# Delta rule: the block transfers begun by GpSimd pair by pair, the merges 19 turns later, more buffers for the inverse and its input

## The chip, the core and the metric

The kernel runs on one core of one Trainium2 chip. TensorE (PE) does the matrix products, VectorE (DVE), ScalarE (ACT) and GpSimd (POOL) work element by element, and SyncE (SP) begins transfers and computes nothing. Every engine executes its own instructions strictly in the order in which the program lists them, and waits where an input is not there or a buffer is not free. A transfer runs by itself once an engine has issued it. The metric is the time of one execution in device microseconds (us).

## The reference, cut to what is concerned

The program is a decoder of four layers followed by a second block of two layers. Layers 0 and 3 mix the tokens with a gated delta rule, the others with differential attention and a gated linear recurrence. The change touches the delta rule alone.

```python
def gated_deltanet(u, valid, w_in, conv_w, a_log, dt_bias, norm_w, w_out):
    proj = u @ w_in                     # [.., 1024] -> q, k, v, z: 4 x 1024, beta and a: 8 each
    qkv = jax.nn.silu(causal_depthwise_conv(proj[..., :DN_CONV_CH], conv_w))
    ...
    o = chunk_gated_delta_rule(q, k, v, beta, g)      # 8 heads of 128
    o = rmsnorm(o, norm_w) * jax.nn.silu(z)
    return o.reshape(b, L, DN_V) @ w_out

def chunk_gated_delta_rule(q, k, v, beta, g):
    ...
    a_strict = jnp.where(strict, jnp.einsum("nbhid,nbhjd->nbhij", kb, kc) * decay, 0.0)
    m = a_strict + jnp.eye(CHUNK, dtype=f32)
    u = lax.linalg.triangular_solve(m, vc * bc[..., None], left_side=True,
                                    lower=True, unit_diagonal=True)
    w = lax.linalg.triangular_solve(m, kb * jnp.exp(gc)[..., None], left_side=True,
                                    lower=True, unit_diagonal=True)
    def step(state, xs):                # along the chunks of the sequence
        v_new = ui - jnp.einsum("bhid,bhde->bhie", wi, state)
        o = (jnp.einsum("bhid,bhde->bhie", qi * jnp.exp(gi)[..., None], state)
             + jnp.einsum("bhij,bhje->bhie", attn, v_new))
        ...
```

For each head and each chunk of the sequence a unit triangular matrix `m` has to be inverted (or solved with), and then a state runs along the chunks.

## The kernel before

**The layout.** The sequence has 272 columns: 16 tokens ahead and two blocks of 128. The kernel works with one triangular matrix of 128 by 128 for each head and block, and one of 16 by 16 for the tokens ahead. The eight heads go in four pairs, p = 0 to 3.

**The big products.** The projections to k, v, q and z come as 16 pieces of weights (`_dn`, `DN_ORDER`: k0 k1 v0 q0 k2 v1 q1 k3 z0 v2 q2 v3 q3 z1 z2 z3, where the digit is the pair). `chunk` (L411) loads a piece: SP issues the transfer `wraw` (L415), ACT casts it to a high part `whi` (L418), and DVE subtracts to get the low part `wlo` (L421). `wraw`, `whi` and `wlo` have three buffers each. `mm3` then multiplies each piece in three passes (high by high, low by high, high by low) with 272 columns: these are the large matmuls `pm`, 48 of a piece.

**The small work** of a pair is a task, a Python generator that emits a few instructions and yields. After every eight large matmuls all tasks are asked once; call this a turn. A task that yields n is left alone for n turns. Where a line says `while ...: yield`, the task waits at build time until another task has come so far. Once all is emitted, a scheduler sets the final order on each engine; each engine executes in that order.

A pair goes through these tasks:

- `dn_keys` begins when k of the pair is projected. It works out the decays (`E`, `Dx`, `Dm`) and norms, has PE multiply k by k (`ga`, `gm`, and `ssq` for the norms), and DVE scales the result into `U`, the five triangular matrices of the pair (four of 128 by 128, and those of the 16 tokens ahead). `U` is held in `fx`, fixed buffers made once per stage in `dn_fixed`, with `At`, `vm`, `km` and the inverse `Y`.
- `dn_blocks` inverts the 40 blocks of 16 by 16 on the diagonals. `U` goes to memory (`ud`, L940), the 40 blocks come back one per partition (`X`, L942), and POOL solves them: 15 steps, each a multiply (L952) and a subtract (L953), and a copy (L954) into `yb`. `yb` goes to memory (`yd`, L957) and comes back spread as `U` is (`yc`, L959). SP issues all four transfers.
- `dn_merge` builds the full inverse from those blocks, by 16 to 32 to 64 to 128. DVE masks `yc` into `Ym` and `yw`; PE multiplies (`gp`, then `pp`, three times); DVE and ACT carry the results between them (`gcm`, `gs`, `yt`) and write them into `Y`. The result is `inv[p]`.
- `dn_chain` begins when q of the pair is projected, and from `inv[p]` on runs the state `St` along the chunks (`ksp`, `pv`, `spn`, `po`). `dn_tail` and `proj_out` then normalise, gate by z and project.

The yields set when the steps are emitted: `ud` and `X`, 6 turns on the solve, 10 turns on `yd` and `yc`, 8 turns on the merge, if the pairs before have come far enough (`solved` counts the pairs whose chain has read its inverse). Pair 2 and 3 further wait with their `U` for the inverse two pairs back, because `U` has two buffers, and the merge of p waits until the chain of p-1 has read `Y`, of which there is one.

The changed functions stand below as they are before.

Of the kernel before, what the change touches and what calls it, by code (L numbers as in the profile page):

```python
# [9 lines left out]
F32 = mybir.dt.float32  # L10
# [7 lines left out]
P = 128  # L18
# [3 lines left out]
T = NM + NX  # L22
# [278 lines left out]
class Prog:  # L301
# [232 lines left out]
    def _dn(self, s, layer, last, e):  # L534
# [14 lines left out]
        self.solved = 0  # L549
# [73 lines left out]
    def dn_fixed(self):  # L623

        d1, V = self.d1, self.V
        self.fx = []
        for i in range(2):
            t = dict(U=d1.tile([P, 5, P], F32, name=f"U{i}"), At=d1.tile([48, 48], F32, name=f"Atm{i}"),
                     vm=d1.tile([48, P], F32, name=f"vm{i}"), km=d1.tile([48, 2, P], F32, name=f"km{i}"),
                     Y=d1.tile([P, 4, P], F32, name="Y") if i == 0 else self.fx[0]["Y"])  # L630
            V.memset(t["U"][:, 4, :], 0.0)
            for n in ("At", "vm", "km"):
                V.memset(t[n], 0.0)
            self.fx.append(t)
# [117 lines left out]
    def dn_ssq(self, x, out):  # L752

        sp = self.pst("ssq2")
        self.V.memset(sp[:, 4:5], 0.0)
        sq = self.d2.tile([P, 2, T], F32, tag="sq2", name="sq2", bufs=1)
        self.act(sq, x, AF.Square)
        for h, c in self.M4:
            i = 2 * h + c
            self.colsum(sp[:, i:i + 1], sq[:, h, self.CK[1 + c]])  # L760
        for h in range(2):
            self.mm(sp[self.RH[h], 4:5], sq[:, h, 0:16], self.ones[:, 0:1])
        self.V.tensor_scalar_add(out=out, in0=sp[:, 0:5], scalar1=EPS)

    def dn_keys(self, p, kT, gates, ready, keys):
# [3 lines left out]
        while not ready.done:  # L769
            yield  # L770
        rows, bet, gc, ng = gates
        fx = self.fx[p % 2]
# [26 lines left out]
        while p > 1 and self.inv[p - 2] is None:  # L799
            yield  # L800
        U = fx["U"]
# [12 lines left out]
        yield from self.dn_blocks(U, box)  # L814
        while p and self.solved < p:
            yield
        self.inv[p] = yield from self.dn_merge(U, box[0], fx["Y"])

    def dn_chain(self, p, kT, vT, qT, gates, keys, outs, last):
# [4 lines left out]
        fx = self.fx[p % 2]  # L824
# [44 lines left out]
        for h in range(2):  # L869
# [3 lines left out]
            act(vm[r], kp[r, 3, :], AF.Copy, scale=sk[r, 4:5])  # L873
        while self.inv[p] is None:
            yield
# [59 lines left out]
    def dn_blocks(self, U, box):  # L935

        d2, dd, V, G = self.d2, self.dd, self.V, self.G
        q = self.nc.sync
        ud = dd.tile([5, 129, P], F32, tag="ud", name="ud")
        q.dma_start(out=ud[:, 0:P, :].rearrange("m p c -> p m c"), in_=U)  # L940
        X = d2.tile([40, 16, 16], F32, tag="X", name="X", bufs=1)
        q.dma_start(out=X, in_=bass.AP(ud.tensor, ud.offset, [[2064, 40], [P, 16], [1, 16]]))  # L942
        yb = d2.tile([40, 16, 2, 16], F32, tag="yb", name="yb", bufs=1)
        yield 6
# [10 lines left out]
        yield 10  # L955
# [4 lines left out]
        box.append(yc)  # L960
        yield 8
# [979 lines left out]
```

## Time and profile before

| | |
|---|---|
| Time, median of 3 runs | 2557.94 us |
| lowest and highest of them | 2555.87 and 2562.32 us |
| the profiled execution, its own time | 2559.32 us |
| its span in the trace | 2557.1 us |
| PE busy | 2496.0 us, 98% of the span |
| DVE busy | 2011.3 us, 79% |
| ACT busy | 1468.4 us, 57% |
| POOL busy | 121.5 us, 5% |

How to read the views: all times are microseconds from the start of the span, unless marked ns. The windows view gives each engine's busy time in a stretch, with the count of its instructions in brackets; its last three columns are the granted clock of PE as a share of its full 2.4 GHz, the busy share of the transfer engines, and GB/s. The waits view lists for an engine what it stood waiting for: the waiting instruction, what released it, microseconds in all, how many times, and the longest. The timeline lists instructions in order: start, duration, engine (SPq is the queue of SP that issues transfers), line, operation, result and operands, and in square brackets the idle time of the engine just before and what ended it. Where several alike follow each other they are one row with x and their count. The names in the rows are those of the program with buffer numbers left out. The two delta-rule stages lie at 12 to 198 us and at 1034 to 1217 us of the span.

### The profile page before, as it was taken

The page shows a single profiled execution, that of the slowest core. Times are in us where ns is not written, and L with a number is a line of the kernel's source. Part 1 is how long each engine was busy: PE and PEld are TensorE (multiplying, and loading weights), DVE is VectorE, ACT ScalarE, POOL GpSimd, SP SyncE. Part 2 cuts the span into 40 slices and gives each one's busy share as a digit, 9 for nine tenths or more (in the row PEclk, how much of TensorE's full clock was granted, in tenths as well). Part 3 has the DMA queues.
Part 4 walks back from the last instruction along what each step waited for, and adds up shares of the span by engine and source line. Part 5 has one row for each costly group of instructions (what it writes and reads, how often), then busy time and mean ns, then how long its engine had stood idle before and what let it go on. Part 6 is the DMA issues. An engine that isn't in the chain of part 4 may idle for free.

```text
span 2557.1 us, 53813 instructions
## 1 busy us (share of the span) xinstructions
PE 2496.0 (98%) x21942; PEld 2424.1 (95%) x21942; DVE 2011.3 (79%) x4433; ACT 1468.4 (57%) x2568; POOL 121.5 (5%) x280
## 2 busy tenths in 40 slices
PE   8899999999999999979999999999999999999998
PEld 8789999999999999978999999999878999999998
DVE  8678967779879986857896787886766977986765
ACT  8776445674457644767754554654664545545544
POOL 1420001000000000242000000000000000000000
PEclk9899999999999999989999999999999999999999
DMA  4326755347545764333785575564414785874553
GB/s 174 114 93 233 287 177 184 124 174 264 198 148 167 262 248 165 123 109 108 271 312 186 207 273 177 175 239 153 153 60 154 269 312 188 307 299 168 175 191 114
DMA packets 89576, 494.54 MB, mean 193 GB/s; under 512 B 18449, under 2 KB 28337, under 8 KB 33265
## 3 DMA queue, kind: packets, MB, share of 16 engines
q1 hardware_dynamic: 89328, 491.10, 54.3%
q8 instruction: 173, 2.83, 0.4%
q14 instruction: 75, 0.61, 0.1%
HBM read 485.10 MB, written 5.96 MB: 192 GB/s over the span
## 4 chain that ended last, share of the span: by engine, by line
PE 83%; DVE 6%; POOL 4%; ACT 3%; DMA 2%; issue 1%; SPq 0%; POOLq 0%; DVEq 0%; ACTq 0%
PE pm L392 77%; POOL yb L953 2%; POOL t L952 2%; DVE wlo L421 1%; PE o L392 1%; ACT L359 1%; DMA wraw<-dnA 1%; DMA X<-ud 1%; PE sp L392 1%; ACT whi L418 1%; PE oT L402 0%; PE ssq L392 0%; DMA ud<-U 0%; DMA yd<-yb 0%; PE ga L392 0%
## 5 line engine op out<-in xcount | busy, mean ns | idle before, releaser
L418 ACT CAST whi<-wraw 128x1024 fp32r<-128x1024 f32 (+1 forms) x767 | 770.9, 1034 | 567.5 <-PE pm L392 321.1
L421 DVE TENSOR_TENSOR wlo<-wraw,whi 128x512 fp32r<-128x512 f32 x1511 | 981.8, 691 | 123.0 <-ACT whi L418 121.4
L392 PE MATMUL pm<-ul,whi 128*128 128x272 f32 (+3 forms) x2856 | 826.1, 290 | 0.4 <-DVE ul L353 0.4
L392 PE MATMUL pm<-uh,whi 128*128 128x272 f32 (+3 forms) x2856 | 822.4, 289 | 3.6 <-ACT uh L359 1.9
L392 PE MATMUL pm<-uh,wlo 128*128 128x272 f32 (+3 forms) x2856 | 823.6, 289 | 0.4 <-DVE wlo L421 0.2
L392 PEld LDWEIGHTS pm<-uh,whi 128*128 128x128 f32 (+1 forms) x2856 | 541.1, 190 | 9.1 <-issue 2.5
L392 PEld LDWEIGHTS pm<-uh,wlo 128*128 128x128 f32 (+1 forms) x2856 | 540.8, 190 | 7.2 <-issue 4.3
L392 PEld LDWEIGHTS pm<-ul,whi 128*128 128x128 f32 (+1 forms) x2856 | 540.9, 190 | 6.6 <-issue 3.0
L392 PE MATMUL pm<-hh,wlo 128*128 128x256 f32 (+1 forms) x1904 | 538.9, 283 | 0.0
L392 PE MATMUL pm<-hh,whi 128*128 128x256 f32 (+1 forms) x1904 | 538.8, 283 | 0.0
L392 PE MATMUL pm<-hl,whi 128*128 128x256 f32 (+1 forms) x1904 | 537.8, 282 | 0.0
L392 PEld LDWEIGHTS pm<-hl,whi 128*128 128x128 f32 x1904 | 359.2, 189 | 0.0
L392 PEld LDWEIGHTS pm<-hh,wlo 128*128 128x128 f32 x1904 | 358.4, 188 | 0.0
L392 PEld LDWEIGHTS pm<-hh,whi 128*128 128x128 f32 x1904 | 358.1, 188 | 0.0
L392 PE MATMUL pm<-vh,whi 128*128 128x256 f32 x912 | 251.3, 277 | 0.3 <-DVE t L356 0.3
L392 PE MATMUL pm<-vh,wlo 128*128 128x256 f32 x912 | 251.1, 277 | 0.3 <-DVE wlo L421 0.2
L392 PE MATMUL pm<-vl,whi 128*128 128x256 f32 x912 | 251.2, 276 | 0.0
L1395 DVE SCALAR_TENSOR_TENSOR wmod<-wmod,crow 128x1024 f32<-128x1024 f32 x144 | 173.8, 1217 | 0.1
L392 PEld LDWEIGHTS pm<-vh,whi 128*128 128x128 f32 x912 | 171.0, 188 | 0.6 <-DVE t L356 0.5
L392 PEld LDWEIGHTS pm<-vh,wlo 128*128 128x128 f32 x912 | 170.6, 188 | 1.0 <-DVE wlo L421 0.7
L392 PEld LDWEIGHTS pm<-vl,whi 128*128 128x128 f32 x912 | 171.1, 188 | 0.0
L356 DVE TENSOR_TENSOR h<-h,pm 128x272 f32<-128x272 f32 (+1 forms) x192 | 82.2, 430 | 83.2 <-PE pm L392 82.6
(464 smaller groups left out, 3060.9 us busy)
## 6 DMA issues: line engine op xcount, KB each, us to landing
wraw<-mlp SPq DMA_DIRECT2D x128, 1024.0 KB, 4.9
wmod<-wmod SPq DMA_DIRECT2D x72, 1024.0 KB, 6.2
wraw<-f1i SPq DMA_DIRECT2D x66, 1024.0 KB, 4.9
wraw<-f2i SPq DMA_DIRECT2D x44, 1024.0 KB, 4.8
wraw<-dnA SPq DMA_DIRECT2D x32, 1024.0 KB, 5.1
wraw<-f1o SPq DMA_DIRECT2D x24, 1024.0 KB, 4.8
wraw<-f2o SPq DMA_DIRECT2D x16, 1024.0 KB, 4.9
wraw<-daA SPq DMA_DIRECT2D x12, 1024.0 KB, 5.0
```

What stands on the lines that cost most here:

```text
L356: self.V.tensor_tensor(out=out, in0=a, in1=b, op=op)
L359: i = self.S.activation(out=out, in_=a, func=func, **k).ins
L392: self.PE.matmul(out=out, lhsT=lhsT, rhs=rhs, start=start, stop=stop)
L418: self.S.copy(out=hi[:, k], in_=raw[:, k])
L421: self.V.tensor_sub(out=lo[:, k], in0=raw[:, k], in1=hi[:, k].bitcast(F32))
L952: G.tensor_tensor(out=o, in0=X[:, 0:k, k:k + 1].broadcast_to([40, k, n]), in1=Y[:, k:k + 1, k:16].broadcast_to([40, k, n]), op=ALU.mult)
L953: G.tensor_tensor(out=Y[:, 0:k, k:16], in0=Y[:, 0:k, k:16], in1=o, op=ALU.subtract)
L1395: i = self.V.scalar_tensor_tensor(out=junk, in0=w[:, k, :], scalar=1.0, in1=c[:, r, :], op0=ALU.mult, op1=ALU.mult, accum_out=m[:, j:j + 1])
```

## The change

The four block transfers of a pair (`ud`, `X`, `yd`, `yc`) are issued by POOL instead of SP (`q = nc.gpsimd`). `U` has four buffers, one for each pair, and `Y` has two; `At`, `vm` and `km` keep two. The wait of `U` for the inverse two pairs back is gone. Two counters are new: `read` says how many chains have read what `dn_keys` made for their pair, and `dn_keys` of pair p begins only when pair p-2 has done so; `blocked` says how many pairs have gone through `dn_blocks`, and the `X` load of a pair is not emitted before the pair ahead is through. The yields change: `ud`, 2 turns on `X`, the solve, `yd` and `yc` together, and 11 + 8 = 19 turns on the merge. The merge of pair p waits until the chain of p-2 has read its inverse and the merge of p-1 is done. The square `sq2` in the tails takes its buffer from the tag `yf` instead of one of its own.

```diff
         chains, outs, self.ms = [], [], {}
-        self.solved = 0
+        self.solved = self.read = self.blocked = 0
         self.inv, keys, f = [None] * 4, [[] for _ in range(4)], {}
...
         self.fx = []
-        for i in range(2):
-            t = dict(U=d1.tile([P, 5, P], F32, name=f"U{i}"), At=d1.tile([48, 48], F32, name=f"Atm{i}"),
-                     vm=d1.tile([48, P], F32, name=f"vm{i}"), km=d1.tile([48, 2, P], F32, name=f"km{i}"),
-                     Y=d1.tile([P, 4, P], F32, name="Y") if i == 0 else self.fx[0]["Y"])
+        for i in range(4):
+            t = dict(self.fx[i - 2]) if i > 1 else dict(
+                At=d1.tile([48, 48], F32, name=f"Atm{i}"), vm=d1.tile([48, P], F32, name=f"vm{i}"),
+                km=d1.tile([48, 2, P], F32, name=f"km{i}"), Y=d1.tile([P, 4, P], F32, name=f"Y{i}"))
+            for n in ("At", "vm", "km") if i < 2 else ():
+                V.memset(t[n], 0.0)
+            t["U"] = d1.tile([P, 5, P], F32, name=f"U{i}")
             V.memset(t["U"][:, 4, :], 0.0)
-            for n in ("At", "vm", "km"):
-                V.memset(t[n], 0.0)
             self.fx.append(t)
...
         self.V.memset(sp[:, 4:5], 0.0)
-        sq = self.d2.tile([P, 2, T], F32, tag="sq2", name="sq2", bufs=1)
+        sq = self.d2.tile([P, 2, T], F32, tag="yf", name="sq2", bufs=1)
         self.act(sq, x, AF.Square)
...
         RH, ck = self.RH, self.CK
-        while not ready.done:
+        while not ready.done or self.read < p - 1:
             yield
         rows, bet, gc, ng = gates
-        fx = self.fx[p % 2]
+        fx = self.fx[p]
         mneg = self.dc("mneg")
...
         yield
-        while p > 1 and self.inv[p - 2] is None:
-            yield
         U = fx["U"]
...
         box = []
-        yield from self.dn_blocks(U, box)
-        while p and self.solved < p:
+        yield from self.dn_blocks(p, U, box)
+        while p and (self.solved < p - 1 or self.inv[p - 1] is None):
             yield
...
         on, om = outs
-        fx = self.fx[p % 2]
+        fx = self.fx[p]
         while len(keys) < 5 or self.solved < p - 1:
...
             act(vm[r], kp[r, 3, :], AF.Copy, scale=sk[r, 4:5])
+        self.read = p + 1
         while self.inv[p] is None:
...
-    def dn_blocks(self, U, box):
+    def dn_blocks(self, p, U, box):
         d2, dd, V, G = self.d2, self.dd, self.V, self.G
-        q = self.nc.sync
+        q = self.nc.gpsimd
         ud = dd.tile([5, 129, P], F32, tag="ud", name="ud")
         q.dma_start(out=ud[:, 0:P, :].rearrange("m p c -> p m c"), in_=U)
+        yield 2
+        while self.blocked < p:
+            yield
         X = d2.tile([40, 16, 16], F32, tag="X", name="X", bufs=1)
...
         yb = d2.tile([40, 16, 2, 16], F32, tag="yb", name="yb", bufs=1)
-        yield 6
         t = d2.tile([40, 15, 16], F32, tag="t16", name="t16", bufs=1)
...
         G.tensor_copy(out=yb[:, :, 1, :], in_=Y.rearrange("p a b -> p b a"))
-        yield 10
         yd = dd.tile([40, 16, 2, 16], F32, tag="yd", name="yd")
...
         box.append(yc)
+        yield 11
+        self.blocked = p + 1
         yield 8
...
```

**SP in the first stage, from the weight loads of the first pieces on.** Before:

```order
L415 DMA wraw<-dnA 128x2048 x6
L940 DMA ud<-U_201 128x5x128
L415 DMA wraw<-dnA 128x2048
L942 DMA X<-ud 40x16x16
L940 DMA ud<-U_210 128x5x128
L942 DMA X<-ud 40x16x16
L957 DMA yd<-yb 40x512
L415 DMA wraw<-dnA 128x2048
L959 DMA yc<-yd 128x5x32
L957 DMA yd<-yb 40x512
L415 DMA wraw<-dnA 128x2048
L959 DMA yc<-yd 128x5x32
```

After, with the weights of the output projection (`dno`) and of what follows it:

```order
L539 DMA dnc<-dnc 128x320
L415 DMA wraw<-dnA 128x2048 x15
L415 DMA wraw<-dno 128x2048 x4
L415 DMA wraw<-mlp 128x2048 x3
L1384 DMA crow<-crow 128x2048
```

The block transfers stood among the weight loads, and now SP's queue holds loads alone through the whole stage.

**POOL at the start of the first stage.** `t_628` and `t_548` are the scratch of the solve; `U_208` and `U_217` in the rows of after are the matrices of pair 0 and pair 1. Before:

```order
L947 MEMSET yb 40x16x16
L948 MEMSET yb 40x16
L952 ISA
L952 TENSOR_TENSOR t_628<-X,yb 40x15
L953 TENSOR_TENSOR yb<-yb,t_628 40x15
```

After:

```order
L949 MEMSET yb 40x16x16
L950 MEMSET yb 40x16
L940 DMA ud<-U_208 128x5x128
L945 DMA X<-ud 40x16x16
L954 ISA
L954 TENSOR_TENSOR t_548<-X,yb 40x15
L940 DMA ud<-U_217 128x5x128
L955 TENSOR_TENSOR yb<-yb,t_548 40x15
```

And further on in after, from the last step of pair 0's solve to the first of pair 1's (`t_777`):

```order
L955 TENSOR_TENSOR yb<-yb,t_548 40x15
L945 DMA X<-ud 40x16x16
L956 COPY yb<-yb 40x16x16
L958 DMA yd<-yb 40x512
L960 DMA yc<-yd 128x5x32
L949 MEMSET yb 40x16x16
L950 MEMSET yb 40x16
L954 TENSOR_TENSOR t_777<-X,yb 40x15
```

POOL held solves only; now the issues stand among their steps, with the `ud` of pair 1 behind the first multiply of pair 0, and the `X` of pair 1 at the end of pair 0's solve.

**PE around the first matmul of pair 1's merge in the first stage** (`gp<-yw`; `po`, `ksp` are pair 0's chain, `ga`, `gm`, `ssq` products and norms of keys, `vp` a transposition for a chain, `pm` the large matmuls). Before:

```order
L392 MATMUL po<-vr,At 128x128
L392 MATMUL po<-St_1406,qT 128x128
L392 MATMUL ssq_1544<-ones,sq_1546 32x1 x16
L392 MATMUL ssq_1544<-ones,sq_1546 16x1 x2
L392 MATMUL pm<-ul,whi 128x272
L392 MATMUL pm<-uh,wlo 128x272
L392 MATMUL pm<-uh,whi 128x272
L392 MATMUL pm<-ul,whi 128x272
L392 MATMUL pm<-uh,wlo 128x272
L392 MATMUL pm<-uh,whi 128x272
L392 MATMUL gp<-yw,U_210 32x32 x16
L392 MATMUL pm<-ul,whi 128x272
```

After:

```order
L392 MATMUL ssq_1344<-ones,sq_1346 32x1 x16
L392 MATMUL ssq_1344<-ones,sq_1346 16x1 x2
L392 MATMUL po<-vr,At 128x128
L392 MATMUL po<-St,qT 128x128
L392 MATMUL ga<-qT,kT 128x128 x4
L392 MATMUL gm<-qT,kT 16x16 x2
L392 MATMUL gp<-yw,U_217 32x32 x16
L392 MATMUL pm<-ul,whi 128x272
L392 MATMUL pm<-uh,wlo 128x272
L392 MATMUL ksp<-St_1382,kT 128x128 x2
L402 MATMUL vp<-ident,vT 128x128 x4
L392 MATMUL pm<-ul,whi 128x272
```

The merge stood behind the whole chain of pair 0; it now stands between the chain's steps, 71 large matmuls behind the first matmul of merge 0, where it had 111. Up to the first matmul of merge 0 there are 331 large matmuls before and 336 after. The next distances after are 92 and 133 in the first stage, and 79, 77 and 131 in the second.

## Rows read from the trace of the kernel before

**Rows 1.** Windows view, first delta-rule stage: stretch, length, PE, PEld, DVE, ACT, POOL, clock.

```profile
12.10:198.30 186.20, 174.57 (x2044) 156.70 (x2045) 138.29 (x398) 144.57 (x309) 52.97 (x130) 0.95 0.35 118
```

**Rows 2.** Waits view of PE, 20 to 205: total us, times, longest.

```profile
PE gp L392 <- ACT yt L359: 5.3, 2, 5.1
PE gp L392 <- DVE raw L559: 3.1, 1, 3.1
PE pp L392 <- ACT gs L1027: 1.8, 1, 1.8
```

**Rows 3.** Waits view of PE, 1030 to 1220.

```profile
PE gp L392 <- ACT yt L359: 12.4, 1, 12.4
PE ksp L392 <- ACT St L888: 2.0, 1, 2.0
PE pp L392 <- ACT gs L1027: 0.7, 1, 0.7
```

**Rows 4.** Windows view, the stretches right behind four of those waits.

```profile
71.40:76.50 5.10, 5.10 (x90) 4.89 (x91) 5.00 (x15) 3.71 (x6) 4.34 (x9) 0.68 0.01 3
89.10:93.20 4.10, 4.09 (x25) 3.72 (x27) 0.00 (x0) 2.70 (x4) 0.00 (x0) 0.50 0.84 348
124.50:131.20 6.70, 6.70 (x36) 5.66 (x36) 3.47 (x11) 4.58 (x10) 0.00 (x0) 0.50 0.26 89
1115.10:1120.60 5.50, 5.50 (x32) 5.01 (x33) 0.00 (x0) 3.79 (x8) 0.00 (x0) 0.50 0.38 161
```

**Rows 5.** Timeline of ACT, the casts ahead of the two longest waits.

```profile
87.43 1.04 ACT L418 CAST whi<-wraw 128x1024 fp32r<-128x1024 f32 x1 [5.48 <-DMA wraw<-dnA]
...
1113.40 1.04 ACT L418 CAST whi<-wraw 128x1024 fp32r<-128x1024 f32 x1 [12.96 <-DMA wraw<-dnA]
```

**Rows 6.** Timeline of SP, second stage, 1105 to 1109.

```profile
1105.80 0.29 SPq L957 DMA_DIRECT2D yd<-yb  x1
...
1108.02 1.41 SPq L415 DMA_DIRECT2D wraw<-dnA  x3
```

**Rows 7.** Timeline of DVE, the first mask of two merges.

```profile
70.61 0.20 DVE L356 TENSOR_TENSOR Ym<-yc,dnc 48x48 f32<-48x48 f32 x1 [3.28 <-DMA yc<-yd]
...
122.48 0.20 DVE L356 TENSOR_TENSOR Ym<-yc,dnc 48x48 f32<-48x48 f32 x1 [4.51 <-DMA yc<-yd]
```

**Rows 8.** Timeline of SP, the four block transfers of pair 3, first stage.

```profile
129.21 0.37 SPq L940 DMA_DIRECT2D ud<-U  x1
131.74 0.31 SPq L942 DMA_DIRECT2D X<-ud  x1
...
149.17 0.29 SPq L957 DMA_DIRECT2D yd<-yb  x1
150.92 0.37 SPq L959 DMA_DIRECT2D yc<-yd  x1
```

**Rows 9.** Tile view of `yb`, POOL: ns min/median/max, first and last start, forms.

```profile
L953 POOL TENSOR_TENSOR yb<-yb,t x120: 213/314/3382, 50.2 to 1172.1; 40x15 f32<-40x15 f32 x16, 40x28 f32<-40x28 f32 x16, 40x39 f32<-40x39 f32 x16, 40x48 f32<-40x48 f32 x16
...
L954 POOL COPY yb<-yb x8: 595/763/1071, 64.2 to 1172.7; 40x256 f32<-40x256 f32 x8
```

**Rows 10.** View of the transfers: count, KB each, median us from issue to landing.

```profile
yc<-yd SPq DMA_DIRECT2D x8, 80.0 KB, 2.1
```

**Rows 11.** Timeline of PE, the first matmuls of merge 0 in both stages.

```profile
71.37 0.45 PE L392 MATMUL gp<-yw,U 32*32 32x32 f32 x32 [3.11 <-DVE raw L559]
...
1090.23 0.45 PE L392 MATMUL gp<-yw,U 32*32 32x32 f32 x32
```

**Rows 12.** Timeline of DVE: the last write of `U`, pairs 0 and 1, then pair 0 again.

```profile
41.27 0.47 DVE L353 SCALAR_TENSOR_TENSOR U<-gm,sv,Dm 16x16 f32<-16x16 f32 x2
...
49.00 0.47 DVE L353 SCALAR_TENSOR_TENSOR U<-gm,sv,Dm 16x16 f32<-16x16 f32 x2
...
1062.22 0.47 DVE L353 SCALAR_TENSOR_TENSOR U<-gm,sv,Dm 16x16 f32<-16x16 f32 x2
```

**Rows 13.** Chain of waits, its unbroken piece behind the first stage: start, us, what, count.

```profile
265.54 154.31 PE pm L392 x1222
```

## The prediction

> **What bounds the kernel now.** Read first the page's shares and its forty slices: TensorE (PE) is busy 98% of the span, so only a stretch in which PE waits or runs slowly can give time back. The change touches the two delta-rule stages alone. Read there the windows view: the first stage lasts 186.2 us from its first gate matmul to its output projection, with PE busy for 174.57 us and a mean granted clock of 0.95 [rows 1]. Both numbers leave something: PE waits and PE at half clock.
>
> The waits view of PE says where. In the first stage there are three waits of weight, 5.1, 3.1 and 1.8 us [rows 2]; in the second three more, 12.4, 2.0 and 0.7 us [rows 3]. They sum to 25.1 us. Behind four of them the windows view shows PE busy without a gap at a lower granted clock, that is partly or wholly at 1.2 instead of 2.4 GHz [rows 4]: 5.1 us at 0.68, 4.1 at 0.50, 6.7 at 0.50, 5.5 at 0.50. Each loses its length times (1 - clock): 1.6 + 2.05 + 3.35 + 2.75 = 9.75 us. **All that these stages can give back is 25.1 + 9.8 = 34.9 us.**
>
> Now the causes. The releaser named for the waits of 5.1 and 12.4 is ScalarE (ACT). ACT itself stood idle 5.48 and 12.96 us for a weight load `wraw<-dnA` [rows 5], with the merge's small copies queued behind the cast that needs it. The load was late because SyncE (SP) issues in order: it stood with `yd` until GpSimd's solve ended at 1105.80, then with `yc` until that had landed, and issued the next three weight loads from 1108.02 on [rows 6]. The 2.0 us wait is the same, behind the `yd` of the last pair. So SP's queue causes 5.1 + 2.05 + 12.4 + 2.75 + 2.0 = 24.3 us. The other 10.6 us come from merges that stand too early in the order: VectorE (DVE) waits 3.28 and 4.51 us for `yc` to land [rows 7] and PE with it.
>
> **The change, part by part.** *SP loses the block transfers.* Sixteen issues per stage leave its queue; the order of SP shows the weight loads standing one behind the other. What then holds a load is the release of its buffer by ACT and DVE, as in every other stage. The 24.3 us go. What is late next is the block chain itself, below.
>
> *GpSimd (POOL) gets them.* No transfer in the trace of before is begun by POOL, so this cost has to be bounded. Let i be POOL's time for one issue, and d = i - 0.3 what the transfer lands later than with SP, whose issue takes 0.29 to 0.37 us [rows 8]. Lower end: i = 0.3, as SP. Upper end: 3.38 us, the longest instruction of POOL's solves, of a kind whose median is 0.31 us [rows 9]. Below SP's price nothing speaks for it. I take **i = 1.0, d = 0.7**, near POOL's copies of one block tile (0.595 to 1.071 us) [rows 9]: like an issue, a short job of POOL whose length depends on what DVE does meanwhile.
>
> One pair's chain today: `ud` issue to `X` issue 2.53, `X` to `yd` 17.43 (2.1 landing, 15.3 solve), `yd` to `yc` 1.75 [rows 8], `yc` to landing 2.1 [rows 10]: 23.8 us. Behind the landing, DVE's two masks take 0.8 us until PE's first merge matmul (70.61 to 71.37) [rows 7, 11].
>
> The Trainium skill, page DMA: Bandwidth & Descriptors, section Anatomy of one DMA — SWDGE (gpsimd) path, fits a POOL-issued transfer with 2.0 us plus its bytes over 436 GB/s, of which the issue is small. By that the four transfers would take, by my estimate, 2.75 + 2.1 + 2.2 + 2.2 = 9.2 us and the sum would stay near the whole 34.9 us. No row here can show it.
>
> *POOL's order in the first stage.* U of pair 0 is ready at 41.74 and of pair 1 at 49.47 [rows 12]. The order puts pair 1's `ud` behind the first solve instruction of pair 0, so POOL holds there until 49.47, a wait of 1.2 us at my price; behind it stand 14.8 us of solve and pair 1's `X`. `yc` of pair 0 lands at 49.47 + i + 14.8 + i + 1.75 + d + 2.1 + d = 71.5. Pair 1's `X` is already there, so its `yc` follows after i + 0.45 (two clears of the block, put by the 0.31 us of a solve step [rows 9]) + 15.3 + 1.75 + d, plus the difference of the ends: 17.5 + i + d = 19.2, at 90.7. Pairs 2 and 3 have their `ud` and `X` in the chain: 22.2 + i + 3d = 25.3 each, at 116.0 and 141.3. In the second stage U of pair 0 is ready at 1062.69 [rows 12]; the same sum without the wait gives 1091.3, 1110.5, 1135.8 and 1161.1.
>
> *PE's order.* Work between merges is priced by count. A 272-column matmul takes 154.31 / 1222 = 0.126 us in the unbroken chain [rows 13]. 768 of them are 97 us; the first stage without its losses is 186.2 - 10.0 - 7.0 = 169.2 us, so its small matmuls are 72 us, which I spread by their counts. From the first matmul of merge 0 to that of merge 1 now stand 71 large ones (111 before), then 92, then 133; with their small ones 18.3, 25.8 and 29.4 us. In the second stage 79, 77 and 131 give 18.9, 23.3 and 28.2. Ahead of merge 0 now stand five more large matmuls (0.6 us) and 24 more small ones, pair 2's products and norms (I put 1.8 us on these). So PE comes to it some 2.4 us later than its 68.26 (71.37 less 3.11) [rows 11], at 70.7, and in the second stage 1.8 us later than 1090.23 [rows 11], at 1092.0.
>
> *New waits* (landing + 0.8 against PE's arrival): first stage 72.3 against 70.7, 1.6 us; 91.5 against 90.6, 0.9; then 116.8 against 117.3 and 142.1 against 146.7, none. Second stage 0.1, 0.3, 2.0 and none. Sum 4.9 us. For the three over 0.5 us I charge the least clock loss seen behind a wait, 1.6 us each [rows 4]: 4.8. **New losses 9.7 us.**
>
> *The rest* I cost at nothing. Two more U and a second Y add two memsets on DVE per stage, before its first wait. `sq2` now shares the buffer of `yf`, so a square on ACT can wait for a split on DVE; both are under 1 us and the tails come late. U no longer waits for the inverse two pairs back, which pulls pair 2's products forward past 75 large matmuls, over 9 us: cover for POOL, no work. Without these covers each is worth 1 or 2 us.
>
> **The sum.** 34.9 - 9.7 = 25.2 us from 2559.32, the profiled execution's own time (span 2557.1): **2534.1 us**. That execution lies 1.4 us over the median of the runs, inside their spread, and I make no allowance for it. A measurement of this kernel can tell about 0.3%, 7.7 us, from no change.
>
> **The rivals.** *The waits change hands.* With i = 1.5 the new waits are 3.6, 1.9 and 1.5 us, then 3.1, 1.3 and 4.0: 15.4 us and six clock losses, 25 us, a gain of 9.9. With i = 2.0 they are 28.4 us and seven losses of 1.6, 39.6 us in all: 4.7 slower. Between 1.6 and 2.2 nothing measurable is left: 2552 to 2567 us. For it: every pair pays four issues on one in-order engine. Against: PE arrives early at only two or three of the eight merges at my price.
>
> *POOL becomes the bound, and the kernel slower.* Place: the four issues of each pair, in line with the solves. Three of them move 640 pieces each (`ud` 512 bytes, `X` 64, `yc` 128), and should POOL take time for each piece, or be held up by DVE as in its 3.38 us instruction, i is 2.2 or more. From there PE waits at every merge: with i = 2.5 the waits are 44.3 us and eight clock losses 12.8, 57 in place of 34.9, so 2582; with 3.38 they are 72.4 and 12.8, so 2610. It decides from about i = 2.2. For it: POOL's solve steps do stretch to over 3 us, and DVE is busy for 138.29 of the 186.2 us [rows 1]. Against: the median of 120 such steps is 0.31 us [rows 9].
>
> The Trainium skill, page SBUF — State Buffer, section SBUF: two separate sides, warns of exactly this: a transfer begun on GpSimd starves while DVE holds the port pair that they share, and should be begun elsewhere. The stretched instructions agree with a shared port; whether an issue suffers as they do, no row here shows.
>
> *It doesn't do what it says:* the weight loads stay late though SP is free, because buffers come free late. That the ring holds three loads speaks for it; that ACT had nothing to do for 12.96 us while three loads stood unissued [rows 5, 6] speaks against. It would keep 24 us of loss, pay 9.7 and lose 10.6: about 2558.
>
> **How the numbers follow.** Forecast (i from 0.3 to 1.5, 2524 to 2550): 0.61. Waits change hands (2550 to 2567): 0.15, of which a little still counts as faster. POOL bound (2567 to 2610): 0.22. Not as it says: 0.02. Faster by over 0.3%: 0.61 + 0.04 = 0.65; within: 0.13; slower: 0.22. The range goes from 2522 (no new loss and some small waits gone) to 2580 (i near 2.5), which leaves about 0.04 below and 0.14 above.
>
> **What would show it.** Right: no ACT idle on `wraw<-dnA` over 2 us in the stages; stages near 171 us; POOL's issues near 1 us; PE waits at merges of 1 to 3 us. Wrong first in POOL's row: issues of 2 us or more, `yc` of pair 3 landing after 150 in the first stage, and PE waiting at every `gp`.

## The result and the profile after

The changed kernel takes 2582.44 us (median; 2580.32 to 2583.52). The kernel before, beside it, takes 2559.15 us. The ratio is 1.0092, with an interval from 1.0072 to 1.0111: it became slower by about 23 us. Forecast were 25 us less.

The loss lies in the two delta-rule stages alone. One account serves for all kernels below: PE's idle time, plus its busy time times (1 - granted clock), summed from the windows view over slices of 2 us from 12 to 252 and from 1030 to 1270. For the kernel before it gives 27.5 us of idle time and 10.2 us of clock, 37.8 in all (the prediction counted 34.9, the large ones alone). For the changed kernel it gives 43.1 and 16.5, 59.6 in all. The difference is 21.8 us; that of the two spans, 2578.6 and 2557.1, is 21.5.

The windows view of the first stage, with the columns of [rows 1], over the same stretch. PE is now busy 9 us less in it, and the stage is not over at its end:

```profile
12.10:198.30 186.20, 165.60 (x1970) 147.79 (x1969) 129.79 (x387) 140.59 (x301) 69.40 (x146) 0.94 0.33 111
```

The part of the forecast that concerns SP came true. The timeline of SP shows weight loads alone, ten in one run:

```profile
35.71 115.39 SPq L415 DMA_DIRECT2D wraw<-dnA  x10
```

ACT no longer waits for a weight load in either stage; before, such waits were 5.48 and 12.96 us [rows 5] and 22.6 us in all.

The waits view of PE, first stage (20 to 240) and second (1030 to 1260), answers [rows 2, 3]:

```profile
PE gp L392 <- DVE Dm L353: 6.6, 1, 6.6
PE kp L402 <- DVE qf L764: 6.4, 1, 6.4
PE pom L392 <- DVE U L353: 4.7, 1, 4.7
...
PE pvm L392 <- ACT vm L359: 7.5, 1, 7.5
PE pv L392 <- DVE rr L353: 7.3, 1, 7.3
PE gp L392 <- DVE Dm L353: 6.5, 1, 6.5
```

Only two of these six stand at a merge. In the other four PE waits for quite different work: a transposition, an output, a correction of the state. What they share is seen on DVE. This is its timeline, the first mask of each merge of the first stage, to be laid beside [rows 7]:

```profile
75.10 0.20 DVE L356 TENSOR_TENSOR Ym<-yc,dnc 48x48 f32<-48x48 f32 x1 [7.67 <-DMA yc<-yd]
...
96.04 0.20 DVE L356 TENSOR_TENSOR Ym<-yc,dnc 48x48 f32<-48x48 f32 x1
...
123.75 0.20 DVE L356 TENSOR_TENSOR Ym<-yc,dnc 48x48 f32<-48x48 f32 x1 [8.23 <-DMA yc<-yd]
...
158.69 0.20 DVE L356 TENSOR_TENSOR Ym<-yc,dnc 48x48 f32<-48x48 f32 x1 [7.58 <-DMA yc<-yd]
```

DVE stands at the masks for 52.0 us in both stages, at seven of the eight; before, it was 11.3 us at three. While it stands, nothing behind it goes on: the evictions of the large matmuls, which free PE's result buffers, the steps of the chains, and the next `U`. The waiting PE instruction is whichever needs one of these first.

Two rows of DVE just behind the mask of 123.75 show the worst of them, the `U` of pair 3:

```profile
124.79 1.11 DVE L353 SCALAR_TENSOR_TENSOR U<-ga,sv,Dx 128x128 f32<-128x128 f32 x4
125.82 0.47 DVE L353 SCALAR_TENSOR_TENSOR U<-gm,sv,Dm 16x16 f32<-16x16 f32 x2
```

So pair 3's transfers cannot start before pair 2's have ended. The timeline of POOL, from pair 2's `ud` to pair 3's, says the same from the other side (its 4.03 us of idle time end with DVE):

```profile
94.91 0.86 POOL L940 DMA_DIRECT2D ud<-U  x1
98.60 0.89 POOL L945 DMA_DIRECT2D X<-ud  x1 [2.83 <-DMA ud<-U]
103.43 0.21 POOL L954 TENSOR_TENSOR t<-X,yb 40x15 f32<-40x15 f32 x1 [3.94 <-DMA X<-ud]
...
118.75 0.58 POOL L958 DMA_DIRECT2D yd<-yb  x1 [0.29 <-POOL yb L956]
121.16 0.90 POOL L960 DMA_DIRECT2D yc<-yd  x1 [1.84 <-DMA yd<-yb]
...
126.59 0.86 POOL L940 DMA_DIRECT2D ud<-U  x1 [4.03 <-DVE raw L559]
```

It also shows POOL idle inside its own chain: it waits for the landing of `ud` before it can issue `X`, for `X` before it can solve, and for `yd` before it can issue `yc`. In that time it cannot solve for another pair.

The price of an issue stands in the tile views of `ud`, `X`, `yd` and `yc` (ns, least, median, most):

```profile
L940 POOL DMA_DIRECT2D ud<-U x8: 865/866/1011, 42.7 to 1158.4; - x8
L945 POOL DMA_DIRECT2D X<-ud x8: 890/891/922, 46.6 to 1161.7; - x8
L958 POOL DMA_DIRECT2D yd<-yb x8: 548/577/584, 68.8 to 1181.3; - x8
L960 POOL DMA_DIRECT2D yc<-yd x8: 881/897/905, 72.5 to 1185.8; - x8
```

And from issue to landing, in the view of the transfers (median us in the last column), beside 2.1 for `yc` with SP [rows 10] and 2.5 for `ud` (129.21 to 131.74 [rows 8]):

```profile
ud<-U POOLq DMA_DIRECT2D x8, 320.0 KB, 3.2
yd<-yb POOLq DMA_DIRECT2D x8, 80.0 KB, 2.7
yc<-yd POOLq DMA_DIRECT2D x8, 80.0 KB, 2.6
X<-ud POOLq DMA_DIRECT2D x8, 40.0 KB, 4.1
```

### The profile page after: what moved, and what is told of

Its sections match the earlier page's. It is cut to its first block, busy times and chain, and to the rows that moved or that the text cites. A ratio compares the mean times of both kernels' runs of the same rounds, so it can differ in the third digit from the quotient of the medians.

```text
span 2578.6 us, 53849 instructions
## 1 busy us (share of the span) xinstructions
PE 2502.2 (97%) x21942; PEld 2430.1 (94%) x21942; DVE 2009.5 (78%) x4437; ACT 1467.8 (57%) x2569; POOL 150.9 (6%) x312
## 4 chain that ended last, share of the span: by engine, by line
PE 82%; DVE 5%; POOL 4%; ACT 3%; DMA 3%; issue 2%; SPq 0%; DVEq 0%; POOLq 0%; ACTq 0%
PE pm L392 76%; POOL t L954 2%; POOL yb L955 2%; DVE wlo L421 1%; PE o L392 1%; ACT whi L418 1%; ACT L359 1%; DMA yd<-yb 1%; PE sp L392 1%; DMA X<-ud 1%; DMA yc<-yd 1%; DMA ud<-U 0%; DMA crow<-crow 0%; PE ssq L392 0%; PE oT L402 0%
## 5 line engine op out<-in xcount | busy, mean ns | idle before, releaser
L392 PEld LDWEIGHTS pm<-uh,whi 128*128 128x128 f32 (+1 forms) x2856 | 543.0, 190 | 10.7 <-issue 4.0
```

Source lines behind the costliest of these rows:

```text
L392: self.PE.matmul(out=out, lhsT=lhsT, rhs=rhs, start=start, stop=stop)
```

## The experiments

Theory A: the time goes where DVE reaches a mask before `yc` has landed. The chain of a pair became longer, since its four transfers are dearer and stand in line on POOL, and the masks moved ahead in the order. Its rivals are named with each run. The masks' places are counted in evictions of the large matmuls that stand ahead of them on DVE: before 11, 16, 19, 26 in the first stage, after 10, 14, 18, 23. (In the expectations of e2, e3, e6 and e10 the third and fourth places of the change, of e3 and e5, and of e10 are one lower; counted on the timeline of DVE they are as given here.)

The times, with the ratio to the kernel before in the same comparison and its interval, the account of losses, DVE's idle time until `yc` (in both stages) and ACT's until a weight load:

| kernel | median us | ratio | PE idle + clock | DVE for `yc` | ACT for `wraw` |
|---|---|---|---|---|---|
| before | 2559.15 | 1 | 37.8 | 11.3 | 22.6 |
| the change | 2582.44 | 1.0092 (1.0072 to 1.0111) | 59.6 | 52.0 | 0 |
| e1, issued by SP | 2564.97 | 1.0026 (1.0006 to 1.0046) | 45.7 | 15.3 | 18.3 |
| e2, before, issued by POOL | 2568.84 | 1.0043 (1.0027 to 1.0060) | 43.1 | 31.7 | 0 |
| e3, merges 5 turns later | 2566.43 | 1.0046 (1.0024 to 1.0068) | 41.0 | 34.2 | 1.0 |
| e4, half on SP, half on POOL | 2570.31 | 1.0040 (1.0014 to 1.0066) | 48.5 | 43.1 | 3.0 |
| e5, e3 and e4 together | 2548.49 | 0.9950 (0.9935 to 0.9966) | 29.3 | 22.9 | 3.7 |
| e6, as e5, 8 turns later | 2544.24 | 0.9925 (0.9902 to 0.9949) | 30.6 | 17.0 | 12.4 |
| e7, the change, masks on POOL | 2557.11 | 0.9974 (0.9959 to 0.9989) | 37.0 | 0 | 0 |
| e8, e6 and a second `X` | 2530.63 | 0.9897 (0.9872 to 0.9921) | 10.1 | 8.3 | 2.5 |
| e9, e5 with masks on POOL | 2546.36 | 0.9945 (0.9927 to 0.9963) | 23.4 | 0 | 0 |
| e10, the buffers alone | 2570.41 | 1.0047 (1.0026 to 1.0068) | 46.2 | 10.7 | 23.2 |
| e11, e8, all by SP | 2559.50 | 1.0004 (0.9986 to 1.0021) | 38.3 | 0 | 28.4 |
| e12, e8, all by POOL | 2555.75 | 0.9980 (0.9962 to 0.9998) | 38.2 | 28.5 | 3.1 |

The account is that of one profiled execution, the median that of all runs. Span less account lies between 2513.9 and 2519.3 us for every kernel but e9 (2527.6), so the account explains the differences of the spans to some 5 us.

**The parts of the change, one by one.** First the queue is undone (e1), then the queue alone is changed (e2), then the buffers alone (e10).

e1 puts back SP and leaves the rest of the change:

```diff
-        q = self.nc.gpsimd
+        q = self.nc.sync
```

> The changed kernel with SP issuing the four block transfers as before; order on PE and DVE, buffers and turns stay as in the changed kernel. Theory A (the block chain comes late because a transfer begun by GpSimd costs more from issue to landing: ud 3.4 for 2.5 us, X 4.1 for 2.1, yc 2.6 for 2.1): yc lands some 4 to 5 us earlier for each pair, VectorE's idle time at the masks falls from 52 us to under 25, and in exchange ScalarE again waits for weight loads behind yd: 2555 to 2572 us. Theory B (the new order alone makes the loss, whoever issues): VectorE's idle time at the masks stays over 40 us and the waits for weights come on top: 2590 us or more.

It took 17 us less than the change, at the middle of theory A's range. DVE's wait for `yc` fell to 15.3 us, and ACT's late weights came back. So POOL's queue, not the new order alone, makes most of the loss.

e2 is the kernel before with `q = self.nc.gpsimd` in its `dn_blocks`.

> The kernel before with GpSimd issuing the four block transfers; its order, turns and buffers stay. The masks then stand 1 to 4 evictions later on VectorE than in the changed kernel (at the 11th, 16th, 19th and 26th eviction, against the 10th, 14th, 17th and 22nd). Theory A: the weight loads are on time, yc lands 4 to 5 us later than with SP, and as the masks come 5 to 20 us later than in the changed kernel the idle time at them is about half of its 52 us: 2548 to 2562 us. Theory B (order alone): no loss is left but that of before's early merges, 2535 to 2542 us. Theory C (GpSimd's issues themselves are the loss): 2575 us or more.

Slower than before by 0.43%, between the ranges of A and of C, of which C gives no account of the rows: POOL's issues took 0.55 to 1.02 us here too. The late weights are gone, as theory A had it, and DVE's wait at the masks rose from 11.3 to 31.7 us, more than half of 52. SP's loss was exchanged for one at the masks of about the same size.

e10 is the change with SP's queue and with before's turns:

```diff
-        q = self.nc.gpsimd
+        q = self.nc.sync
...
-        yield 2
-        while self.blocked < p:
-            yield
...
+        yield 6
...
+        yield 10
         yd = dd.tile([40, 16, 2, 16], F32, tag="yd", name="yd")
...
-        yield 11
         self.blocked = p + 1
```

> The kernel before with the change's buffers and waits alone: four U, two Y, a merge no longer waits for the chain of the pair ahead. SP issues, and the turns are those of before (6, 10, 8). The masks then stand at the 11th, 14th, 17th and 23rd eviction of the first stage, where before has them at the 11th, 16th, 19th and 26th. Theory A (the second Y pulls the later merges ahead of their yc): VectorE's idle time at the masks rises from 11 us to over 20 and the weight loads stay late: 2562 to 2576 us. Theory B (the buffers cost nothing, the queue does): 2556 to 2561 us.

The time is that of theory A, its reason only in part. The buffers, with the waits that go with them and `sq2` in the buffer of `yf`, cost 0.47%; the merges did move ahead (masks at 11, 14, 18, 24). But DVE's wait stayed at 10.7 us and the late weights at 23.2. PE's idle time is that of before, 27.7 us, and 18.5 us instead of 10.2 are lost by the clock. Nearly all of that difference lies in the second stage (11.2 us for 3.0). There the kernel before has one long wait of PE (12.4 us [rows 3]) and one stretch at the lower clock behind it (0.50 of the full clock, 1.2 GHz); e10 has three waits, of 4.9, 5.5 and 3.0 us, and such a stretch behind each. The windows view of e10:

```profile
1100.90:1107.00 6.10, 6.07 (x56) 6.01 (x57) 5.99 (x20) 4.49 (x7) 5.08 (x14) 0.50 0.01 3
1118.30:1127.00 8.70, 8.70 (x65) 7.62 (x66) 5.29 (x17) 4.96 (x11) 7.14 (x21) 0.50 0.33 121
1191.50:1199.00 7.50, 7.50 (x124) 6.63 (x124) 4.95 (x15) 2.59 (x10) 0.00 (x0) 0.57 0.21 55
```

The same idle time in more pieces cost more of the clock. Why the new order cuts it into more pieces is not settled.

**The place of the merges and the length of the chain.** e3 leaves all on POOL and emits the merges five turns later (masks at 12, 16, 19, 24):

```diff
         self.blocked = p + 1
-        yield 8
+        yield 13
```

> The changed kernel with the merges 24 instead of 19 turns behind the solve's emission; GpSimd issues. The masks move on VectorE from the 10th, 14th, 17th and 22nd eviction of the first stage to the 12th, 16th, 18th and 23rd. Theory A: VectorE reaches the masks 5 to 10 us later, its idle time there falls from 52 us to under 20, and PE's long waits in the two stages from 41 us to under 18: 2535 to 2552 us. Theory B (a stage lasts as long as GpSimd's chain of four pairs, wherever the merges stand): the waits move behind the last merge and the time stays at 2575 us or more.

It won 12 us by the ratio and 16 by the medians, less than A had it, and theory B is out as well. The waits view of DVE, first and second stage, shows fewer and longer waits:

```profile
DVE Ym L356 <- DMA yc<-yd: 13.4, 1, 13.4
...
DVE Ym L356 <- DMA yc<-yd: 20.8, 3, 15.3
```

Where DVE isn't held at one mask it comes sooner to the next, and is held there. That the chain of pairs, where it runs slower than the distance of their masks, has to be waited for somewhere is argued from this, not shown.

e4 leaves the merges and shortens the chain: `ud` and `X` by SP, `yd` and `yc` by POOL.

```diff
-        q = self.nc.gpsimd
+        q = self.nc.sync
...
+        q = self.nc.gpsimd
         q.dma_start(out=yd, in_=yb)
```

> The changed kernel with ud and X issued by SP, and yd and yc by GpSimd. SP then never waits for the solve, only for U and for the landing of ud. Theory A: ud and X land at SP's prices, 0.9 and 2.0 us less, and GpSimd saves two issues of 0.9 us for each pair, so yc lands some 4 us earlier for the first pair and more for the last: VectorE's idle time at the masks 15 to 30 us instead of 52, 2545 to 2562 us. Theory B (the wait for the landing of yd on GpSimd, 22 us in eight pairs, is what counts): 2572 us or more.

It won 13 us in the ratio, but its median is 8 us above theory A's range, with 43.1 us at the masks where 15 to 30 were expected. The time alone doesn't tell A from B, whose bound of 2572 us is as near; against B speaks e8 below, the fastest of all, in which POOL still begins `yd` and `yc`. `yc` of the first three pairs came 1 to 8 us sooner (masks at 74.18, 95.18 and 116.12), and DVE was there sooner too, at the third by 1.5 us.

e5 has both edits.

> Both edits at once: ud and X by SP, yd and yc by GpSimd, and the merges 24 turns behind the solve's emission. U of pair 3 then stands ahead of pair 2's masks on VectorE, so X of pair 3 is there when GpSimd is free. Theory A (what is lost is lost at masks that VectorE reaches before yc has landed; a queue of its own for yd and yc, landings 4 us earlier and masks later take it away): VectorE's idle time at the masks under 25 us in the eight pairs, PE's long waits under 20 us: 2540 to 2553 us. Theory B (the places bring the waits with them: the later merges only shift them onto the chains and the tails): 2560 us or more.

As theory A has it. Alone the two edits take the ratio from 1.0092 to 1.0046 and 1.0040, so that their sum would give 0.9994; together they give 0.9950, a difference hardly wider than the intervals. By the account the two just add up: 59.6 less 18.6 and 11.1 would be 29.9 us, and 29.3 are left. A shorter chain and later masks are both needed, but that they do more together than apart is not shown.

e6 is e5 with `yield 16`: masks at 13, 17, 19, 26.

> As the run with both edits, with the merges 27 turns behind the solve's emission; the masks stand at the 13th, 17th, 19th and 26th eviction of the first stage, against the 12th, 16th, 18th and 23rd. Theory A: VectorE's idle time at the masks under 12 us, and the tails still in time for the output projection, since before has its last mask at the 26th too: 2532 to 2548 us. Theory B: chains and tails are late, PE waits at the output projection, 2560 us or more.

Within theory A's range, but not clear of e5 (0.25% less with overlapping intervals, and an account of 30.6 us for 29.3), and 17.0 us at the masks where 12 were the most. The rest is a second loss that A knows from SP. Timeline of SP, then of ACT:

```profile
90.65 0.30 SPq L945 DMA_DIRECT2D X<-ud  x1
...
96.15 1.04 ACT L418 CAST whi<-wraw 128x1024 fp32r<-128x1024 f32 x1 [3.77 <-DMA wraw<-dnA]
...
1114.10 1.04 ACT L418 CAST whi<-wraw 128x1024 fp32r<-128x1024 f32 x1 [6.69 <-DMA wraw<-dnA]
```

`X` has one buffer, so SP stands with the next `X` until POOL's solve has left it, with weight loads behind.

e8 gives `X` a second buffer; room for it comes from single buffers of `yc` and `Ym` (their masks now stand at 13, 17, 22, 26).

```diff
-        X = d2.tile([40, 16, 16], F32, tag="X", name="X", bufs=1)
+        X = d2.tile([40, 16, 16], F32, tag="X", name="X", bufs=2)
...
-        yc = d2.tile([P, 5, 2, 16], F32, tag="yc", name="yc")
+        yc = d2.tile([P, 5, 2, 16], F32, tag="yc", name="yc", bufs=1)
...
-        Ym = d2.tile([48, 48], F32, tag="Ym", name="Ym")
+        Ym = d2.tile([48, 48], F32, tag="Ym", name="Ym", bufs=1)
...
-        tri32 = d2.tile([P, P], F32, tag="X", name="tri32", bufs=1)
+        tri32 = d2.tile([P, P], F32, tag="yb", name="tri32", bufs=1)
```

> As the run with half of the transfers on GpSimd and merges 8 turns later, with a second buffer for X (yc and Ym give up theirs, tri32 moves to the buffer of yb). There SP stood with X until the solve of the pair ahead had freed X (90.65 in the first stage), and ACT then waited 3.8 and 6.7 us for a weight load; now X is loaded while GpSimd still solves. Theory A (what is left of the loss is again SP's queue, and masks that come before yc): no wait of ACT for wraw over 2 us in the stages, GpSimd goes from solve to solve, VectorE's idle time at the masks under 10 us: 2530 to 2541 us. Theory B (one buffer of yc and Ym holds GpSimd's queue and the masks instead): 2544 us or more.

All as theory A has it: 2530.63 us, 1.03% under the kernel before, and the best of all. The ratio's gain on e6 is only 0.28%, about as wide as the intervals, but the account falls by 20.5 us. The new buffers also moved the third mask from the 19th to the 22nd eviction, and no run separates this from the second `X`. POOL now goes from solve to solve. Its timeline, the `yd` of pairs 1 to 3, shows them 18.9 and 18.3 us apart, where the change has 27.8 and 33.0 (90.98, 118.75, 151.78):

```profile
87.99 0.58 POOL L959 DMA_DIRECT2D yd<-yb  x1 [0.29 <-POOL yb L956]
...
106.92 0.58 POOL L959 DMA_DIRECT2D yd<-yb  x1 [0.29 <-POOL yb L956]
...
125.21 0.58 POOL L959 DMA_DIRECT2D yd<-yb  x1 [0.29 <-POOL yb L956]
```

Of the 37.8 us that the two stages lose in the kernel before, 10.1 are left.

**The queue again, in this best order.** e11 and e12 keep every other edit of e8 and let one queue issue all four transfers, SP in e11 and POOL in e12. PE's merges and DVE's masks keep their places.

```diff
-        q = self.nc.gpsimd
         q.dma_start(out=yd, in_=yb)
```

> The kernel with the second X and the merges 8 turns later, with all four block transfers begun by SP. PE, VectorE and ACT keep the order that they had with half on GpSimd. Theory A (two separate losses: SP's queue, and masks ahead of yc; only the second is gone here): ACT waits again for weight loads behind yd, 10 to 25 us in the two stages, VectorE hardly for yc: 2542 to 2558 us. Theory B (the late masks alone make the gain, the queue hardly matters): 2528 to 2538 us.

```diff
-        q = self.nc.sync
+        q = self.nc.gpsimd
...
-        q = self.nc.gpsimd
         q.dma_start(out=yd, in_=yb)
```

> The same kernel with all four block transfers begun by GpSimd, as in the change. Theory A (GpSimd's dearer transfers hurt only where a mask comes before yc; yc at about 75, 95, 120 and 146 in the first stage against masks that VectorE reaches at about 83, 104, 131 and 152): VectorE's idle time at yc under 8 us, no late weights: 2528 to 2540 us. Theory B (four transfers a pair on GpSimd's queue bound the stage wherever the masks stand): 2550 us or more.

e11 loses the whole gain, e12 about four fifths of it. The waits view of ACT in e11, first and second stage:

```profile
ACT whi L418 <- DMA wraw<-dnA: 14.8, 1, 14.8
...
ACT whi L418 <- DMA wraw<-dnA: 13.3, 1, 13.3
```

The time of e11 is 1.5 us above theory A's range and ACT's waits, 28.4 us, are 3.4 above theirs, but the reason is the one given: a whole solve stands in SP's queue, ahead of a weight load. In e12 theory A fell and theory B held: the waits view of DVE, first and second stage, has masks ahead of `yc` again.

```profile
DVE yw L356 <- DMA yc<-yd: 8.8, 1, 8.8
...
DVE Ym L356 <- DMA yc<-yd: 8.8, 2, 8.3
DVE yw L356 <- DMA yc<-yd: 8.0, 1, 8.0
```

POOL begins to solve pair 2 at 100.16, 10.5 us behind the `yd` of pair 1; in e8 it begins at 91.99, 4.0 us behind the `yd` of 87.99. The difference is the issue and the flight of pair 2's `ud` and `X`, for which POOL stands by (5.0 us of idle time).

**DVE's part by itself.** e7 is the change with the masks worked out by POOL; e9 is e5 with the same edit.

```diff
-        def blocks(out, y, mask, w, p=P, m=4):
+        def blocks(out, y, mask, w, p=P, m=4, eng=self.V):
...
-            tt(out.rearrange("p m (b a) -> p m b a", b=nb), bc(y, 2, nb), bc(bc(mask, 1, m), 3, w), ALU.mult)
+            eng.tensor_tensor(out=out.rearrange("p m (b a) -> p m b a", b=nb), in0=bc(y, 2, nb), in1=bc(bc(mask, 1, m), 3, w), op=ALU.mult)
...
-        blocks(Ym.unsqueeze(1), yc[0:48, 4:5, 0, :], dc("in16")[0:48, 0:3], 16, 48, 1)
+        blocks(Ym.unsqueeze(1), yc[0:48, 4:5, 0, :], dc("in16")[0:48, 0:3], 16, 48, 1, eng=G)
...
-            blocks(yw[:, :, t, :], yc[:, 0:4, t, :], dc("hf16"), 16)
+            blocks(yw[:, :, t, :], yc[:, 0:4, t, :], dc("hf16"), 16, eng=G)
```

> The changed kernel with the three masks of a merge (Ym and the two halves of yw) worked out by GpSimd instead of VectorE, so that no landing of yc holds VectorE; turns and transfers stay. Theory A (half of the loss is VectorE held at a mask, with evictions and the next U behind it): VectorE waits for no yc, U of pair 3 is no longer late, and PE waits only where it reaches a merge: 2555 to 2570 us, 12 to 27 us less than the changed kernel. Theory B (only the length of the block chain counts): PE waits as long as before at the merges and GpSimd's chain gets longer by the masks: 2580 us or more.

As theory A has it, by the ratio 1.2% under the change. `yc` is issued at nearly the same times (74.24, 97.03, 123.68 and 153.20 for 72.53, 93.41, 121.16 and 156.06), so the chain is no shorter but for the last pair. Yet the loss falls from 59.6 to 37.0 us, because DVE goes on. PE's waits of over 1 us are at merges alone now. Its timeline, the first stage:

```profile
81.14 0.65 PE L392 MATMUL gp<-yw,U 32*32 32x32 f32 x32 [9.79 <-POOL yw L978]
...
127.89 0.45 PE L392 MATMUL gp<-yw,U 32*32 32x32 f32 x32 [1.50 <-POOL yw L978]
```

> Three edits at once: ud and X by SP, yd and yc by GpSimd, merges 24 turns behind the solve's emission, and the masks of a merge on GpSimd. Theory A (the edits add up as far as they remove waits for yc): VectorE waits for no yc, PE only at the first merge of each stage, where the masks stand behind 14 steps of the next solve: 2540 to 2550 us. Theory B (GpSimd in order: masks and solves hold each other): 2555 us or more.

As theory A has it: no wait for `yc` on DVE, and PE's only long waits are at the first merge of each stage, 6.79 and 9.10 us, where the masks stand behind part of the next solve. Yet it is no faster than e5 (0.9945 against 0.9950); its profiled execution, the slowest of its four runs, spent some 11 us more than that of e5 outside what the account counts, and why is open.

## Why the prediction was wrong, by its own steps

- **What bounds the kernel, and what can be had** was right. The two stages lose 35 to 38 us; e8 got 28 of them back.
- **SP loses the block transfers: 24.3 us** was right. ACT waits for no weight load after the change, and e11 brings the loss back in the order of e8.
- **POOL's price of an issue, i = 1.0 us**, was right: 0.55 to 1.01 us, and never stretched.
- **d, the later landing, 0.7 us for each transfer,** was right for a transfer that flew nearly alone: `ud` landed after 3.1 us for 2.5, `yc` after 2.6 for 2.1, two of the eight `X` after 2.75 and 2.82 for the 2.1 used, and from `yd` to `yc` it took 2.41 us for 1.75 [rows 8]. What the sum left out is what flies beside it. The median `X` took 4.1 us, and from `yd` to `yc` it took up to 4.28 us in the first stage. The trace of before had shown it for a transfer begun by SP: `X` of pair 0 took 4.96 us to POOL's first step, where the prediction priced every pair by pair 3 (131.74 to 133.85):

```profile
44.70 0.35 SPq L942 DMA_DIRECT2D X<-ud  x1
...
49.66 0.43 POOL L952 TENSOR_TENSOR t<-X,yb 40x15 f32<-40x15 f32 x1 [48.44 <-DMA X<-ud]
```

A pair wholly in line on POOL took 27.7 us from landing to landing (96.04 to 123.75), for 25.3 in the prediction.

- **The new waits, 4.9 us,** is the step that failed; the six long waits of PE above sum to 39.0 us. It set the landing of `yc` plus 0.8 us against PE's arrival at the merge, and both ends were wrong. PE isn't the first to arrive: it would have come to merge 0 at 77.86 - 6.64 = 71.2, where the prediction has 70.7, but DVE was at the mask at 75.10 - 7.67 = 67.4. From there on evictions and `U` stood still, so that PE stopped elsewhere in four of the six, and DVE then had a backlog: PE's `gp` came 2.8 us behind the mask, not 0.8 behind the landing. And the landings were worked out as if the block chain went its own pace. The `U` of pair 3 stands behind the mask of pair 2 on DVE, so a late `yc` makes the next one late: the four landings of the first stage were put at 71.5, 90.7, 116.0 and 141.3, and the masks began at 75.1, 96.0, 123.8 and 158.7. e7 prices DVE's standing alone at 22.6 us of the account.
- **The clock behind waits, 4.8 us,** was mis-sized with the waits: 16.5 us.
- **More buffers at nothing** was wrong: e10 makes them 0.47% by themselves. The distances of the merges on PE were counted rightly, but that the new buffers draw masks ahead on DVE, to 14, 18 and 23 from 16, 19 and 26, was not looked at. With SP's queue the waits at the masks did not grow by it (10.7 us in e10); the loss there is in the clock.
- **The rival "POOL becomes the bound"** came to 57 us of loss and 2582 at i = 2.5. The time agrees and its stated cause does not, since i is 0.9; its sign of a `yc` of pair 3 after 150 came true (158.7) without it. It is the waits for landings, in line on POOL, and the loop through DVE that make the stage as slow.
- **The two pages.** The Trainium skill, page SBUF — State Buffer, section SBUF: two separate sides, warned that a transfer begun by GpSimd starves while DVE holds the shared port, as it does in some instructions, an fp32 copy in SBUF among them. Its advice, to begin such transfers elsewhere, agrees with e1, 17 us faster than the change; its reason is not seen here. In the windows view, the flights of the four `yd` of the first stage (the third busy time is DVE's, the last number GB/s of all transfers):

```profile
68.81:72.40 3.59, 2.41 (x54) 2.01 (x52) 0.00 (x0) 1.41 (x4) 0.55 (x1) 1.00 0.68 267
90.98:93.40 2.42, 2.42 (x22) 1.87 (x21) 1.85 (x5) 1.08 (x4) 0.58 (x1) 1.00 0.13 34
118.75:121.16 2.41, 2.41 (x19) 2.14 (x17) 0.00 (x0) 2.37 (x5) 0.57 (x1) 1.00 0.46 170
151.78:156.06 4.28, 3.51 (x65) 3.13 (x63) 0.00 (x0) 1.76 (x4) 0.58 (x2) 1.00 0.70 258
```

The two slow ones fell into stretches in which DVE did nothing and all transfers together moved 258 and 267 GB/s; the one beside a busy DVE was fast. DVE ran five `SCALAR_TENSOR_TENSOR` there, no copy, so the case that the page names is not tested here. The Trainium skill, page DMA: Bandwidth & Descriptors, section Anatomy of one DMA — SWDGE (gpsimd) path, gave 9.2 us for the four, by the prediction's estimate; the medians above sum to 12.6, of which `X` has the largest part that the estimate lacks (4.1 for 2.1).

## What to carry to other kernels

An instruction that waits for a far transfer is priced on the engine that executes it, by what is queued behind it there, not on the engine that the result is meant for; look above all for a loop, where what is queued behind feeds the next transfer. A queue that waits inside its own chain (issue, landing, issue) doesn't serve two purposes: neither SP with weight loads behind, nor POOL with solves behind, could carry all four transfers, and the split of them, with a buffer that lets the next load fly during the solve, was worth more than either (2530.63 us against 2559.50 and 2555.75 with the same buffer). An extra buffer isn't free because it does no work: it changes the order that the scheduler makes, and in e10 that cost 0.47% with no more idle time. And price a transfer by more than one of its rows: the quiet one is the cheapest.

## What was not expected of the hardware

A transfer begun by POOL held POOL for 0.55 us (`yd`, 40 rows) to 1.01 us, steadily, and where little else flew it landed 0.5 to 0.8 us later than one begun by SP. More than that went with the traffic beside it. In the windows view, the flights of three `X` of the changed kernel, then two of the kernel before, begun by SP (length second, GB/s of all transfers last):

```profile
66.97:72.04 5.07, 4.25 (x68) 3.76 (x66) 0.46 (x4) 3.22 (x6) 2.10 (x3) 1.00 0.72 235
129.94:133.85 3.91, 3.91 (x27) 3.79 (x26) 1.41 (x6) 1.94 (x7) 0.89 (x1) 0.79 0.13 15
1130.23:1132.98 2.75, 2.49 (x86) 2.24 (x89) 2.75 (x11) 1.70 (x9) 0.89 (x1) 1.00 0.16 15
...
44.70:49.66 4.96, 4.96 (x75) 4.60 (x74) 4.70 (x20) 4.90 (x12) 0.00 (x0) 1.00 0.74 223
131.74:133.85 2.11, 2.11 (x17) 1.80 (x17) 0.93 (x2) 1.88 (x6) 0.00 (x0) 1.00 0.21 19
```

The second of them is an exception, slow with little traffic; and a `yd` flew through 170 GB/s in 2.41 us. That the rest is the sharing of the transfer engines is argued from such stretches; no run here separates it from other causes.
